# Splitting the conv half of the output weights on GpSimd instead of ScalarE and VectorE, in the late stages of an RWKV-7 and short-convolution block

## The chip, the core and the metric

The kernel runs on one core of a Trainium2 chip. The metric is the device time of one launch in microseconds (us). The engines are called as the profile calls them: PE (TensorE matmul) with its weight loads PEld, DVE (VectorE), ACT (ScalarE), POOL (GpSimd) and SP (SyncE, which issues most DMAs).

## The reference

One layer is applied to 128 context tokens and to 2048 latent tokens. Both are RMS-normalised, modulated and projected by one matrix. Half of the channels go through RWKV-7 mixing in two directions (a recurrence over the tokens, 8 heads of 64), the other half through a gated short convolution; both halves are gated, joined and sent through one output matrix. What this case touches is the end:

```python
ya = ya.astype(x.dtype) * jax.nn.silu(g_a)
yb = b_gate * _short_conv(c_gate * u_conv, lp['conv_w'], is_latent) * jax.nn.silu(g_b)
u = jnp.concatenate([ya, yb], axis=-1) @ lp['w_out']
return x + gate * u, s_final
```

The inner width is 1024: rows 0 to 511 of `w_out` belong to `ya` (the attention half) and rows 512 to 1023 to `yb` (the conv half). All is float32.

## The kernel before, in words

The kernel has three phases. Phase 1 makes the projections and the whole conv half of the mix, and writes them to DRAM (`mixT` holds the mix, transposed). Phase 2 runs the recurrence in chunks of 64 tokens; phase 3 is the output projection with the final norm.

**Phase 2** has 17 stages (0 to 16): 16 for latent tokens, and the context as stage 15. Each stage has two groups of 8 units (one group for each direction). Its work is cut into parts: `partW` (matmuls psF and psG, masked by DVE at L1041 and L1048, copied by ACT at L831), `partU` (psU, psW), `partB` (psX, copied by ACT at L829; psE, whose one half DVE masks at L1109 and whose other half ACT copies at L831 into the tile E) and `partS` (psS, the recurrence itself, with DVE at L1147). A round does `partS` of stage s beside W, U and B of stage s+1; the order of the pieces is a string written out by hand (ROUND, and ROUND_END from stage 14 on), and the matmuls of phase 2 are chained in that order on PE. `finish` (psT, L1195 to L1217) ends a block of the mix. GpSimd's own work in phase 2 is a triangular solve for each stage (`solve`, L935 to L955); the last one ends before the late stages.

**Phase 3** multiplies tiles of 128 tokens by the output matrix. A float32 matmul there is made of three products of rounded numbers: each operand is split into a rounded part hi (type fp32r) and the rest lo = x - hi, and hi*hi, hi*lo and lo*hi are summed (L1380 to L1382). So every block of 128 rows of weights (k = 0 to 7, of 128x1024) is loaded as `woraw`, rounded into `woh` (`load_k`, L1360) and subtracted into `wol` (L1361); every tile's mix is loaded as `mx`, rounded into `mh` (`load_m`, L1372) and subtracted into `ml` (L1373). CONV is k = 4 to 7, ATT is k = 0 to 3.

**The work done ahead.** `ahead` (L1392) does part of phase 3 in the late stages of phase 2: it splits the four conv blocks of weights, and then the conv half of the mixes of tiles 5 and 6 (AHEAD), multiplies these (psa, 24 matmuls a tile) and keeps the result in `z0`. The tiles that hold the split weights are reused from phase 2: woh4 and wol4 take the place of stage 13's operands, woh5 and wol5 that of stage 14's, so they can be written only when the psF and psG matmuls of that stage are over. The buffers `raw` are two: woraw4 and woraw5 are loaded early, and woraw6, woraw7, mxc5 and mxc6 each take a buffer that an earlier subtraction has released. The attention half is split later, by `tail`, with ACT at L1360 and POOL at L1361.

A scheduler places all these instructions into each engine's one queue; every engine works its queue in order. The DMAs of `woraw` (L1354) and `mx` (L1369) stand in SP's queue between the loads of phase 2, of which those of `fg` (`load_half`, L998 and L1001) are the many.

Of the kernel before, what the change touches and what calls it, by code (L numbers as in the profile page):

```python
# [6 lines left out]
F32 = mybir.dt.float32  # L7
F32R = mybir.dt.float32r
BF16 = mybir.dt.bfloat16
AF = mybir.ActivationFunctionType  # L10
ALU = mybir.AluOpType
# [1328 lines left out]
def phase3(K):  # L1340
    nc, tc, A, S = K.nc, K.tc, K.A, K.S
    V, G, P, T = nc.vector, nc.gpsimd, nc.scalar, nc.tensor
    D = nc.sync.dma_start
    O = Ctx()
    wk = {}
    CONV, ATT = (4, 5, 6, 7), (0, 1, 2, 3)
    TILES = [5, 6, 7, 8, 9, 10, 11, 12, 0, 13, 14, 15, 16, 1, 2, 3, 4]
    AHEAD = TILES[:2]
    z0 = {}

    def load_raw(k):

        raw = O.r.tile([128, 1024], F32, tag="raw", name=f"woraw{k}", bufs=2)
        D(raw[:], A["wout"][k * 128:(k + 1) * 128, :])  # L1354
        return raw

    def load_k(k, hi, lo, eng, raw=None):

        raw = raw or load_raw(k)
        P.copy(hi[:], raw[:])  # L1360
        eng.tensor_tensor(lo[:], raw[:], hi[:].bitcast(F32), ALU.subtract)  # L1361
        wk[k] = (hi, lo)

    def load_m(pool, i, ks, b):

        t0 = i * 128
        a = "c" if ks is CONV else "a"
        mx = O.r.tile([128, 4, 128], F32, tag="raw", name=f"mx{a}{i}", bufs=2)
        D(mx[:], S["mixT"].rearrange("(k p) t -> p k t", p=128)[:, ks[0]:ks[0] + 4, t0:t0 + 128])  # L1369
        mh = pool.tile([128, 4, 128], F32R, tag=f"mh{a}", name=f"mh{a}{i}", bufs=b)  # L1370
        ml = pool.tile([128, 4, 128], F32R, tag=f"ml{a}", name=f"ml{a}{i}", bufs=b)
        P.copy(mh[:], mx[:])  # L1372
        V.tensor_tensor(ml[:], mx[:], mh[:].bitcast(F32), ALU.subtract)  # L1373
        return mh, ml

    def products(ps, ms, cs, ks, start, stop):
        mh, ml = ms
        for n, k in enumerate(ks):
            hi, lo = wk[k]
            T.matmul(ps[:], mh[:, n], hi[:, cs], start=start and n == 0, stop=False)  # L1380
            T.matmul(ps[:], mh[:, n], lo[:, cs], start=False, stop=False)  # L1381
            T.matmul(ps[:], ml[:, n], hi[:, cs], start=False, stop=stop and n == 3)  # L1382

    HALF = [slice(0, 512), slice(512, 1024)]

    def weights():
        O.r = Pool(K, "p3r", "left")
        O.pr = Pool(K, "p3pr", "right", 2, PSUM)
        O.pu = O.pr
        O.raw = [load_raw(k) for k in CONV[:2]]  # L1390

    def ahead():  # L1392
        yield
        for n, k in enumerate(CONV):
            load_k(k, *[K.spare(f"wo{a}{k}", F32R, f"o{k - 3}{m}") if n < 2 else O.r.tile([128, 1024], F32R, name=f"wo{a}{k}") for m, a in enumerate("hl")], V, O.raw[n])
            if n < 2:
                O.raw.append(load_raw(CONV[n + 2]))
            yield
        for i in AHEAD:
            ms = load_m(O.r, i, CONV, 1)  # L1400
            if i not in z0:
                z0[i] = K.spare(f"z0_{i}", F32, "ab2" if z0 else "ab")
            for h in range(2):
                ps = O.pr.tile([128, 512], F32, tag="u", name=f"psa{i}_{h}")
                products(ps, ms, HALF[h], CONV, True, True)
                P.copy(z0[i][:, HALF[h]], ps[:])
                yield

    def tail():
        O.l = Pool(K, "p3l", "right")  # L1410
        for k in ATT:
            load_k(k, *[K.spare(f"wo{a}{k}", F32R, ("o00", "o01", "o30", "o31", "zb")[k * 2 + n]) if k * 2 + n < 5 else O.l.tile([128, 1024], F32R, name=f"wo{a}{k}") for n, a in enumerate("hl")], G)
        gb = O.l.tile([128, 2, 1024], F32, name="gb")
        for s in range(2):
            D(gb[:, s], S["gate"][s:s + 1, :].broadcast_to((128, 1024)))
        fg = O.l.tile([128, 1024], F32, name="fg")
        D(fg[:], A["fg"].broadcast_to((128, 1024)))
        eps = O.l.tile([128, 1], F32, name="eps3")
        V.memset(eps[:], 1e-6)
        yield  # L1420

        def tl(shape, tag, i, dt=F32, b=2):
            return O.l.tile(shape, dt, tag=tag, name=f"{tag}{i}", bufs=b)

        for i in TILES:
            t0 = i * 128
            mc = load_m(O.r, i, CONV, 1) if i not in z0 else None
            assert K.mixed[(i - 1) // 4 if i else None] == (4 if i else 1)
            ma = load_m(O.l, i, ATT, 2)
            xt = tl([128, 1024], "x3", i)  # L1430
            D(xt[:], A["x"][t0:t0 + 128, :])
            z = tl([128, 1024], "z", i)
            s = 1 if i == 0 else 0
            ss = tl([128, 2], "ss", i)
            sq = tl([128, 512], "sq", i, b=1)
            last = i == TILES[-1]
            for n, cs in enumerate(HALF):
                ps = O.pu.tile([128, 512], F32, tag="u", name=f"psu{i}_{cs.start}")
                if mc:
                    products(ps, mc, cs, CONV, True, False)  # L1440
                products(ps, ma, cs, ATT, not mc, True)
                if mc:
                    V.tensor_tensor(z[:, cs], ps[:], gb[:, s, cs], ALU.mult)  # L1443
                else:
                    V.tensor_tensor(z[:, cs], ps[:], z0[i][:, cs], ALU.add)
                    V.tensor_tensor(z[:, cs], z[:, cs], gb[:, s, cs], ALU.mult)
                (V if last else G).tensor_tensor(z[:, cs], z[:, cs], xt[:, cs], ALU.add)  # L1447
                P.activation(sq[:], z[:, cs], AF.Square, accum_out=ss[:, n:n + 1])
            V.tensor_tensor(ss[:, 0:1], ss[:, 0:1], ss[:, 1:2], ALU.add)
            P.activation(ss[:, 0:1], ss[:, 0:1], AF.Sqrt, bias=eps[:], scale=1.0 / 1024)  # L1450
            V.reciprocal(ss[:, 0:1], ss[:, 0:1])
            for cs in HALF if last else [slice(0, 1024)]:
                V.scalar_tensor_tensor(z[:, cs], z[:, cs], ss[:, 0:1], fg[:, cs], ALU.mult, ALU.mult)
                D(S["y"][t0:t0 + 128, cs], z[:, cs])
            yield

    def rest(gen):
        O.pl = Pool(K, "p3pl", "left", 6, PSUM)
        O.pu = O.pl
        for _ in gen:  # L1460
            pass
        for p in (O.pl, O.pr, O.l, O.r):
            p.close()

    K.weights, K.ahead, K.tail, K.rest = weights, ahead, tail, rest


# [43 lines left out]
```

## Time and profile before

| what | value |
|---|---|
| median of 3 runs | 1651.52 us (1651.35 to 1659.19) |
| the profiled execution | 1657.8 us, its span 1656.0 us |
| busy share of the span | PE 93%, PEld 85%, DVE 67%, ACT 46%, POOL 34% |
| mean granted clock of PE | 0.969 |

In the profile, the window views give for a stretch of time the busy us of each engine, the granted clock of PE (1.00 is full speed), the busy share of the DMA engines and GB/s. A timeline's row gives start, length, engine, line, operation, tiles and count, and in brackets the idle time ahead of it with what ended it. Late stages are here those from 1322 us on: psa is worked from 1373.72 to 1393.66 us, and the tiles' own loop of phase 3 starts at 1466.21 us and runs to the end.

### The profile page before, as it was taken

The numbers are of one execution on the slowest core, as the hardware profiler recorded it, in microseconds if no ns is written. First come the engines' busy times: TensorE is split into PE (matmuls) and PEld (weight loads), VectorE is DVE, ScalarE is ACT, GpSimd is POOL, SyncE is SP. The second block draws the span as 40 slices with busy tenths as digits, with TensorE's granted clock in tenths as the row PEclk, the third lists the DMA queues.
The fourth block names the chain that finished last, engine by engine and source line by source line (L and its number), as shares of the span: only waits on it lengthen the run. The fifth ranks groups of instructions, "written<-read, shape, count | busy, mean of one in ns | idle before, by whom it ended". The sixth has DMA issues, their size and how long they took to land.

```text
span 1656.0 us, 42386 instructions
## 1 busy us (share of the span) xinstructions
PE 1538.7 (93%) x17160; PEld 1412.4 (85%) x17160; DVE 1108.4 (67%) x2226; ACT 766.8 (46%) x1623; POOL 569.0 (34%) x1028
## 2 busy tenths in 40 slices
PE   5899999999999999999999899988988888789998
PEld 2899998999999999999988898878887777668886
DVE  5876977784738775658787883576775765574333
ACT  4544565553425353435554013667675665432222
POOL 0011211110102121112765564888888700022221
PEclk8899999999999999999999999999999989889999
DMA  9677767664746465655858768676767643264342
GB/s 377 205 263 249 244 234 276 218 225 178 241 140 208 166 207 183 200 202 186 271 165 270 237 201 239 179 192 180 204 175 195 169 131 102 66 198 160 127 149 93
DMA packets 237988, 327.23 MB, mean 198 GB/s; under 512 B 91288, under 2 KB 191896, under 8 KB 223712
## 3 DMA queue, kind: packets, MB, share of 16 engines
q1 hardware_dynamic: 231840, 318.55, 60.8%
q0 software_dynamic: 1200, 3.93, 0.6%
q8 instruction: 135, 2.21, 0.6%
q10 hardware_dynamic: 4752, 2.04, 0.5%
q14 instruction: 61, 0.50, 0.1%
HBM read 207.92 MB, written 116.54 MB: 196 GB/s over the span
## 4 chain that ended last, share of the span: by engine, by line
PE 47%; DVE 10%; ACT 7%; DMA 4%; issue 3%; POOL 3%; SPq 0%; DVEq 0%; ACTq 0%; POOLq 0%
PE psu L1380 4%; PE psu L1381 4%; PE psu L1382 4%; PE psE L840 3%; PE psS L840 2%; ACT fg L829 2%; PE psX L840 2%; PE psW L840 1%; PE mmg L166 1%; PE mmg L168 1%; PE mmg L167 1%; PE mmc L166 1%; PE mmc L167 1%; PE mmu L167 1%; PE mmu L166 1%
## 5 line engine op out<-in xcount | busy, mean ns | idle before, releaser
L950 POOL TENSOR_TENSOR zt<-zt,ztmp 128x30 f32<-128x30 f32 (+7 forms) x390 | 153.3, 393 | 30.6
L840 PE MATMUL psE<-fg 128*64 128x128 f32 x2176 | 135.8, 278 | 17.4 <-ACT fg L831 15.2
L840 PEld LDWEIGHTS psE<-fg 128*64 128x64 f32 x2176 | 120.8, 139 | 24.1 <-ACT fg L831 17.8
L840 PE MATMUL psS<-sv,E 128*64 128x64 f32 x2176 | 99.5, 235 | 19.3 <-DVE sv L1147 18.4
L840 PEld LDWEIGHTS psS<-sv,E 128*64 128x64 f32 x2176 | 82.5, 144 | 35.5 <-DVE sv L1147 24.4
L329 POOL TENSOR_TENSOR shk<-rawl 128x384 f32<-128x384 f32 (+1 forms) x24 | 24.8, 1033 | 242.9 <-ACT rawl L325 223.8
L829 ACT ACTIVATE fg<-psX 64x512 f32<-64x512 f32 x136 | 80.4, 591 | 44.9 <-PE psX L840 42.8
L1147 DVE TENSOR_TENSOR sv<-psS,pc 64x128 f32<-64x128 f32 x254 | 63.9, 277 | 43.6 <-PE psS L840 41.4
L947 POOL TENSOR_TENSOR ztmp<-ab,zt 128x60 f32<-128x60 f32 (+4 forms) x165 | 85.1, 516 | 12.9
L1447 POOL TENSOR_TENSOR z<-z,x 128x512 f32<-128x512 f32 x32 | 41.7, 1304 | 138.3 <-DVE z L1443 114.8
L329 POOL TENSOR_TENSOR shv<-rawl 128x384 f32<-128x384 f32 (+1 forms) x24 | 20.8, 866 | 164.5 <-ACT rawl L325 164.4
L1041 DVE TENSOR_TENSOR F<-psF,consts 128x512 f32<-128x512 f32 x68 | 44.0, 681 | 46.5 <-PE psF L840 46.5
L831 ACT COPY fg<-psG 64x256 f32<-64x256 f32 x136 | 49.8, 366 | 52.4 <-DVE fg L1048 46.3
L1048 DVE TENSOR_TENSOR fg<-psG,consts 64x256 f32<-64x256 f32 x136 | 57.3, 421 | 24.0 <-ACT fg L831 11.7
L166 PE MATMUL mmc<-h,w 128*128 128x384 f32 (+1 forms) x192 | 64.8, 337 | 5.9 <-ACT q1r L327 4.1
L446 POOL COPY pcs<-pp 128x6 f32<-128x6 f32 (+1 forms) x48 | 21.0, 437 | 139.2 <-ACT pp L435 138.9
L166 PE MATMUL mmg<-h,w 128*128 128x384 f32 (+1 forms) x192 | 64.3, 335 | 3.8 <-ACT q1v L327 3.8
L831 ACT COPY E<-psE 128x256 f32<-128x256 f32 x136 | 48.4, 373 | 37.8 <-DVE E L1109 27.9
L1109 DVE TENSOR_TENSOR E<-psE,consts 128x256 f32<-128x256 f32 x136 | 53.0, 418 | 19.0 <-PE psE L840 17.6
L166 PE MATMUL mmb<-h,w 128*128 128x384 f32 (+1 forms) x192 | 62.9, 328 | 1.5 <-ACT ta L439 1.5
L166 PE MATMUL mmgb<-h,w 128*128 128x384 f32 (+1 forms) x192 | 64.0, 333 | 0.3 <-ACT q1r L327 0.3
L168 PE MATMUL mmg<-h,w 128*128 128x384 f32 (+1 forms) x192 | 64.0, 334 | 0.0
(323 smaller groups left out, 5173.3 us busy)
## 6 DMA issues: line engine op xcount, KB each, us to landing
w<-scr_wsp SPq DMA_DIRECT2D x68, 1024.0 KB, 5.7
scr_wsp<-w SPq DMA_DIRECT2D x34, 1024.0 KB, 4.9
scr_ops<-pair SPq DMA_DIRECT2D x80, 384.0 KB, 4.0
wr<-in_win SPq DMA_DIRECT2D x34, 512.0 KB, 5.9
o<-scr_ops SPq DMA_DIRECT2D x32, 512.0 KB, 6.6
fg<-scr_ops SPq DMA_DIRECT2D x120, 128.0 KB, 3.5
x<-in_x SPq DMA_DIRECT2D x17, 512.0 KB, 8.5
wadas<-in_wada SPq DMA_DIRECT2D x8, 1024.0 KB, 13.5
```

The lines of the kernel that those rows point to most:

```text
L166: T.matmul(ps[:, :n], w[:, 0, k], hh[:, 0, k, :n], start=k == 0, stop=False)
L168: K.dense = T.matmul(ps[:, :n], w[:, 1, k], hh[:, 0, k, :n], start=False, stop=k == 7).ins
L829: P.activation(dst, src, AF.Copy, scale=-1.0)
L831: P.copy(dst, src)
L840: r = T.matmul(*a, start=True, stop=True, **k)
L947: eng.tensor_tensor(tv, ab[:, j:j + 2, j + 2:32].unsqueeze(1).broadcast_to((128, kn, 2, n)), zt[:, :kn, j:j + 2].unsqueeze(3).broadcast_to ...
L950: last = eng.tensor_tensor(zt[:, :kn, j + 2:32], zt[:, :kn, j + 2:32], tv[:, :, r], ALU.subtract).ins
L1048: V.tensor_tensor(g.gs[H[1 - h], g.op, h, us], ps[gi][r, :, 64:128], B.mG[r, g.d].unsqueeze(1).broadcast_to((64, 4, 64)), ALU.mult)
L1147: r = V.tensor_tensor(dst, sp[gi][0:64, q], B.pc[0:64, d, 2 * p:2 * p + 2, c:c + 1].broadcast_to((64, 2, 64)), ALU.mult)
L1380: T.matmul(ps[:], mh[:, n], hi[:, cs], start=start and n == 0, stop=False)
L1381: T.matmul(ps[:], mh[:, n], lo[:, cs], start=False, stop=False)
L1382: T.matmul(ps[:], ml[:, n], hi[:, cs], start=False, stop=stop and n == 3)
```

## The change

`load_k` copies with GpSimd when it is given a `raw` tile, which only `ahead` does, and `ahead` hands GpSimd to it for the subtraction as well; `load_m` gets the engines as arguments, and `ahead` passes GpSimd for both. So twelve instructions move: four casts of 128x1024 (ACT, L1360) and four subtractions of 128x1024 (DVE, L1361), two casts of 128x512 (ACT, L1372) and two subtractions of 128x512 (DVE, L1373), all to POOL. The attention half and the other 15 tiles are as they were. Lines from 1359 on are one higher after the change.

```diff
     def load_k(k, hi, lo, eng, raw=None):
 
+        copy = P.copy if raw is None else G.tensor_copy
         raw = raw or load_raw(k)
-        P.copy(hi[:], raw[:])
+        copy(hi[:], raw[:])
         eng.tensor_tensor(lo[:], raw[:], hi[:].bitcast(F32), ALU.subtract)
...
-    def load_m(pool, i, ks, b):
+    def load_m(pool, i, ks, b, copy=P.copy, eng=V):
...
-        P.copy(mh[:], mx[:])
-        V.tensor_tensor(ml[:], mx[:], mh[:].bitcast(F32), ALU.subtract)
+        copy(mh[:], mx[:])
+        eng.tensor_tensor(ml[:], mx[:], mh[:].bitcast(F32), ALU.subtract)
...
         for n, k in enumerate(CONV):
-            load_k(k, *[...], V, O.raw[n])
+            load_k(k, *[...], G, O.raw[n])
...
-            ms = load_m(O.r, i, CONV, 1)
+            ms = load_m(O.r, i, CONV, 1, G.tensor_copy, G)
```

The scheduler then orders the queues anew. On POOL, behind the last solve, this is the difference (woh4 is the rounded block k = 4, sv are the states that phase 2 clears for stage 15, mhc5 and mlc5 are the two parts of tile 5's mix):

```order
 L955 DMA scr_zt_66<-zt_1124_15938 128x512
+L1361 CAST woh4_17891<-woraw4_17735 128x1024
+L1362 TENSOR_TENSOR wol4_17892<-woraw4_17735,woh4_17891 128x1024
+L1361 CAST woh6_17947<-woraw6_17895 128x1024
+L1362 TENSOR_TENSOR wol6_17948<-woraw6_17895,woh6_17947 128x1024
+L1361 CAST woh7_17998<-woraw7_17933 128x1024
+L1362 TENSOR_TENSOR wol7_17999<-woraw7_17933,woh7_17998 128x1024
 L970 MEMSET sv_1207_17780 64x128 x4
+L1373 CAST mhc5_18060<-mxc5_18058 128x512
 L970 MEMSET sv_1208_17786 64x128 x4
+L1361 CAST woh5_17929<-woraw5_17737 128x1024
+L1374 TENSOR_TENSOR mlc5_18061<-mxc5_18058,mhc5_18060 128x512
```

Blocks 4, 6 and 7 come first, then the parts of tile 5 mixed with the memsets, then block 5; wol5, mhc6 and mlc6 follow.

On DVE, in the round in which stage 13's E is made (psE13 with group and piece), two pieces of the difference show the places of wol6 and mlc5:

```order
 L1109 TENSOR_TENSOR E_1182_17259<-psE13_1_00_17260,consts_9809 128x4x64
 L1109 TENSOR_TENSOR E_1181_17247<-psE13_0_01_17271,consts_9809 128x4x64
-L1361 TENSOR_TENSOR wol6_17948<-woraw6_17895,woh6_17947 128x1024
 L1109 TENSOR_TENSOR E_1182_17259<-psE13_1_01_17282,consts_9809 128x4x64
 L1041 TENSOR_TENSOR F_1190_17359<-psF14_0_0_17341,consts_9809 128x512
```

```order
 L1147 TENSOR_TENSOR sv_1168_16901<-psS13_1_0_17395,pc_10967 64x128
 L1109 TENSOR_TENSOR E_1193_17403<-psE13_0_11_17437,consts_9809 128x4x64
-L1373 TENSOR_TENSOR mlc5_18061<-mxc5_18058,mhc5_18060 128x512
 L1109 TENSOR_TENSOR E_1194_17415<-psE13_1_11_17448,consts_9809 128x4x64
 L1147 TENSOR_TENSOR sv_1167_16899<-psS13_0_0_17389,pc_10967 64x128
```

Each subtraction stood between two masks of E, and is gone from there; the rest keeps its order, but for three masks at L1048, which come one or two places earlier.

On SP, the loads of `woraw6`, `woraw7` and the mixes move against the loads of `fg` for stage 15:

```order
 L987 DMA sv_1188_17336<-scr_vt_60 64x1024
-L1354 DMA woraw6_17895<-in_wout 128x1024
 L1001 DMA fg0_9816<-scr_ops0_57 64x2x128 x4
 L1001 DMA fg1_9817<-scr_ops1_58 64x2x128 x4
+L1354 DMA woraw6_17895<-in_wout 128x1024
+L1001 DMA fg0_9816<-scr_ops0_57 64x2x128 x3
 L1354 DMA woraw7_17933<-in_wout 128x1024
-L1369 DMA mxc5_18058<-scr_mixT_63 128x4x128
-L1001 DMA fg0_9816<-scr_ops0_57 64x2x128 x4
+L1001 DMA fg0_9816<-scr_ops0_57 64x2x128
 L1001 DMA fg1_9817<-scr_ops1_58 64x2x128 x4
-L1369 DMA mxc6_18169<-scr_mixT_63 128x4x128
```

`woraw6` now comes behind the eight loads of fg's first half, `woraw7` stands among those of its second half, and both mixes are loaded later, behind `zc` and the gate loads of a block. On PE, the same 48 products of psa stand at the same place in phase 2's order, at stage 15's psF; those that need mlc5 and wol5 have moved some places back among them.

More of the change, by code (lines that the diff above doesn't have):

```diff
@@ L1394, in ahead @@
         for n, k in enumerate(CONV):
-            load_k(k, *[K.spare(f"wo{a}{k}", F32R, f"o{k - 3}{m}") if n < 2 else O.r.tile([128, 1024], F32R, name=f"wo{a}{k}") for m, a in enumerate("hl")], V, O.raw[n])
+            load_k(k, *[K.spare(f"wo{a}{k}", F32R, f"o{k - 3}{m}") if n < 2 else O.r.tile([128, 1024], F32R, name=f"wo{a}{k}") for m, a in enumerate("hl")], G, O.raw[n])
             if n < 2:
```

## The prediction

> **What bounds the kernel now.** I read the page first, then the busy time by stretches, then the timelines of PE, ACT, DVE and SP in the late stages. Each stretch below runs from one psU to the next, which is one round (columns: length, busy us of PE, PEld, DVE, ACT, POOL with counts, granted clock, DMA share, GB/s).
>
> ```profile
> span 1656.0 us, 42386 instructions
> ```
>
> ```profile
> 1298.80:1322.00 23.20, 21.47 (x585) 19.37 (x580) 18.40 (x45) 15.00 (x32) 15.97 (x35) 1.00 0.69 186
> 1322.00:1353.90 31.90, 25.30 (x586) 21.87 (x583) 20.20 (x47) 20.65 (x40) 0.00 (x0) 0.89 0.47 126
> 1353.90:1394.30 40.40, 38.05 (x632) 31.64 (x630) 18.05 (x45) 21.11 (x42) 1.26 (x8) 0.87 0.37 102
> ...
> 1341.30:1348.10 6.80, 6.13 (x80) 5.00 (x74) 4.43 (x9) 5.63 (x10) 0.00 (x0) 0.50 0.36 98
> ...
> 1355.00:1361.70 6.70, 6.70 (x137) 5.95 (x132) 3.26 (x7) 3.54 (x6) 0.00 (x0) 0.50 0.55 154
> ...
> 1372.00:1375.40 3.40, 3.40 (x39) 2.78 (x29) 0.22 (x1) 2.35 (x5) 0.00 (x0) 0.51 0.63 187
> ```
>
> The first round holds no work of phase 3 and ran at full clock: 23.2 us. The second has the same matmuls (586 against 585) and took 31.9. POOL stood idle in it, while ACT and DVE carried 5.7 and 1.8 us more. In three stretches of 6.8, 6.7 and 3.4 us PE had half its clock. PE's timeline shows where the time goes:
>
> ```profile
> 1298.85 1.20 PE L840 MATMUL psU<-zr,a 32*32 32x32 f32 x64
> ...
> 1308.97 3.71 PE L840 MATMUL psE<-fg 128*64 128x128 f32 x64
> ...
> 1313.54 1.05 PE L840 MATMUL psF<-fg,o 64*64 64x128 f32 x32
> ...
> 1315.00 1.09 PE L840 MATMUL psG<-fg,o 64*64 64x128 f32 x28 [0.19 <-ACT fg L829]
> ...
> 1316.53 1.92 PE L840 MATMUL psE<-fg 128*64 128x128 f32 x32
> ...
> 1322.00 1.20 PE L840 MATMUL psU<-zr,a 32*32 32x32 f32 x64
> ...
> 1332.22 2.84 PE L840 MATMUL psE<-fg 128*64 128x128 f32 x48
> 1336.18 1.09 PE L840 MATMUL psE<-fg 128*64 128x128 f32 x16 [1.12 <-ACT fg L831]
> ...
> 1340.31 1.58 PE L840 MATMUL psF<-fg,o 64*64 64x128 f32 x32 [2.00 <-ACT E L831]
> ...
> 1343.26 1.97 PE L840 MATMUL psG<-fg,o 64*64 64x128 f32 x28 [0.53 <-ACT fg L829]
> ...
> 1346.06 2.94 PE L840 MATMUL psE<-fg 128*64 128x128 f32 x32
> ...
> 1353.25 0.69 PE L840 MATMUL psS<-sv,E 128*64 128x64 f32 x16 [1.57 <-DVE sv L1147]
> 1353.87 1.20 PE L840 MATMUL psU<-zr,a 32*32 32x32 f32 x64
> ...
> 1365.81 2.84 PE L840 MATMUL psE<-fg 128*64 128x128 f32 x48
> 1370.65 1.09 PE L840 MATMUL psE<-fg 128*64 128x128 f32 x16 [2.00 <-ACT fg L831]
> ...
> 1373.15 0.65 PE L840 MATMUL psF<-fg,o 64*64 64x128 f32 x4
> ```
>
> PE is the engine that works through the late stages in order, and four times it waits for 1.12 to 2.00 us on ACT or DVE. The rows of ACT just ahead of these waits say what held it:
>
> ```profile
> 1333.11 1.04 ACT L1360 CAST woh<-woraw 128x1024 fp32r<-128x1024 f32 x1
> ...
> 1338.94 1.04 ACT L1360 CAST woh<-woraw 128x1024 fp32r<-128x1024 f32 x1 [1.89 <-DMA woraw<-in_wout]
> ...
> 1351.33 0.62 ACT L1372 CAST mhc<-mxc 128x512 fp32r<-128x512 f32 x1 [1.02 <-DMA mxc<-scr_mixT]
> ...
> 1367.19 1.04 ACT L1360 CAST woh<-woraw 128x1024 fp32r<-128x1024 f32 x1
> ```
>
> ```profile
> 1351.98 0.69 DVE L1373 TENSOR_TENSOR mlc<-mxc,mhc 128x512 fp32r<-128x512 f32 x1 [1.17 <-ACT mhc L1372]
> 1352.59 0.42 DVE L1109 TENSOR_TENSOR E<-psE,consts 128x256 f32<-128x256 f32 x1
> ```
>
> A cast does not only cost its 1.04 us. The second one stood in ACT's queue for 1.89 us until its weights landed, with copies of E behind it, and PE's psF waited for these. In the same way DVE held a mask of E behind mlc, which waited for mhc, which waited for a load.
>
> **What the change takes away.** The twelve instructions leave ACT and DVE, and with them the waits for DMA in the middle of the recurrence's chain. I price it by comparison with the clean round. There psE came 10.12 us after psU (1308.97 less 1298.85), psF 4.57 after that, the next psU 8.46 after that. In the late rounds the same steps took 10.22, 8.09 and 13.56 us, then 11.94 and 7.34. The excess is 0.10 + 3.52 + 5.10 + 1.82 + 2.77 = 13.3 us up to 1373.15, where psa begins. Of the twelve, all but the cast and the subtraction of tile 6 stand ahead of that point; these two fell beside psa.
>
> Of the 13.3 us, half clock made 0.88 (1.97 against 1.09 for 28 psG), 1.02 (2.94 against 1.92 for 32 psE) and the 1.82 of the step from psU to psE, whose matmuls had no wait of more: 3.7 us. The other 9.6 us are waits and what follows from them. These I count whole, since the first round shows that nothing else in such a round holds PE for long. The half clock follows a wait each time: after the 2.00 us ahead of 1340.31, and after the 1.57 us ahead of 1353.25. Without these waits it should go, but where such a stretch falls may differ from one execution to the next, and the profiled execution is 6.3 us above the median of the timed runs (1657.8 against 1651.52), by what is not shown. So I count half, 1.9 us, and keep 0 and 3.7 for the range.
>
> The Trainium skill (TensorE: Matmul & The Clock Gate, Part 1: The HAM clock gate) has it that a free-running activity window of about 3.4 us decides on half or full clock; the stretches of 6.8, 6.7 and 3.4 us agree as two, two and one of them. By that rule the term is a matter of how the windows fall, anywhere between nothing and all of it.
>
> **What it adds.** POOL now makes all of it, one after another, and SP's queue stands between. The rows for the prices:
>
> ```profile
> L1361 DVE TENSOR_TENSOR wol<-woraw,woh x4: 1173/1225/1226, 1334.2 to 1368.3; 128x1024 fp32r<-128x1024 f32 x4
> L1361 POOL TENSOR_TENSOR wol<-woraw,woh x4: 2336/2346/2778, 1406.5 to 1456.5; 128x1024 fp32r<-128x1024 f32 x4
> ```
>
> ```profile
> L970 POOL MEMSET sv<- x8: 194/196/198, 1364.1 to 1365.4; 64x128 f32 x8
> ```
>
> ```profile
> L935 POOL MEMSET zt<- x13: 524/529/533, 900.7 to 1289.0; 128x512 f32 x13
> ```
>
> ```profile
> L1129 POOL COPY sv<-held x2: 283/285/287, 1402.3 to 1403.3; 64x128 f32<-64x128 f32 x2
> ```
>
> ```profile
> 1335.43 0.34 SPq L1354 DMA_DIRECT2D woraw<-in_wout  x1
> 1335.87 5.20 SPq L1001 DMA_DIRECT2D fg<-scr_ops  x8
> 1341.27 0.43 SPq L1354 DMA_DIRECT2D woraw<-in_wout  x1
> ...
> 1348.36 0.38 SPq L1369 DMA_DIRECT2D mxc<-scr_mixT  x1
> ```
>
> The subtraction takes 2.35 us on POOL against 1.22 on DVE, and I take 1.2 for the half-sized one. No cast runs on POOL before. Twice the memset of 128x512 is 1.06 us, and a two-input subtraction is 2.35: the price c of a cast of 128x1024 lies between them. A copy of 64x128 took 285 ns where a memset of that size took 196, 1.45 times as much, and 1.45 times 1.06 is the 1.5 us I take; it is nearer the memset, since a copy too has less to read than the subtraction.
>
> The Trainium skill (GPSIMD Engine Reference, 4.1 Engine selection) speaks against this change: elementwise work of two inputs belongs on VectorE, as GpSimd is about twice as slow, and with one input it is roughly at line rate. The trace agrees on the first (2.35 against 1.22), and no row shows the second; at the page's 1.2 GHz, 1024 elements would be an estimated 0.85 us, and by that POOL would hardly be late at all and the gain 11.5.
>
> The chain on POOL, in the time of before: woh4 can start when psG of stage 13 ends, at 1332.3, and wol4 ends at 1332.3 + 1.5 + 2.35 = 1336.2. SP now issues woraw6 behind the eight fg loads (5.20 us, from some 1335.2), at 1340.4, and it lands 3.5 us later, as before (1335.43 to 1338.94). wol6 ends at 1347.8. Only then woraw7 can go, with five fg loads queued behind it, which stage 15 reads late; it lands at 1351.3, and wol7 ends at 1355.2. mxc5 lands at 1358.2 (2.97 us, as 1348.36 to 1351.33), and mhc5 ends at 1358.9. With a memset (0.63 for four pieces, estimated at 0.8) woh5 ends at some 1361.2, mlc5 at 1362.4 and wol5 at 1364.8. woh5 waits besides for psG of stage 14, which by then is over.
>
> PE, moved by 13.3, would come to psa at 1360.4. It has four products of woh4 and wol4 (0.23 us each):
>
> ```profile
> 1376.70 0.40 PE L1380 MATMUL psa<-woh,mhc 128*128 128x512 f32 x1
> 1376.93 0.39 PE L1381 MATMUL psa<-wol,mhc 128*128 128x512 f32 x1
> ```
>
> At 1361.3 it then waits 1.1 us for mlc5, does four more and 16 matmuls of phase 2, and waits another 0.9 us for wol5: late by 2.0 us. Each microsecond more for c adds 3.5 us (woh6, woh7, woh5 and half of one for mhc5), so the bounds of c give 0.5 and 5.0. In front of phase 2's matmuls stands psa on PE, so this lateness holds up everything. Tile 6 is not late: PE needs mhc6 some 10 us later, and POOL has 2.7 us to do for it.
>
> **The sum.** 9.6 + 1.9 - 2.0 = 9.5 us; I take 9.2 and leave the rest for waits that show up behind those removed. The profiled execution would go from 1657.8 to 1648.6, and the median from 1651.5 to 1642.3 us. From 1394 on everything hangs on PE and on what PE releases, so all of it moves forward by the same.
>
> **The rivals.** *The clock is not won.* The waits go, but half clock falls elsewhere: none of the 3.7 us comes back, and one more window of half the 6.8 us costs 1.7: 9.6 - 2.0 - 1.7 = 5.9, or 1645.6 us. For it speaks that the 1.57 us wait was enough for 6.7 us at 0.50; against it, that the clean round has waits below half of that and the clock at 1.00.
>
> *POOL is late.* If c is at the subtraction's 2.35, PE waits 5.0 us ahead of psa and falls to half clock there, which costs another 1.9, and none of the old clock term counts: 9.6 - 5.0 - 1.9 = 2.7, or 1648.8 us. The two-input rows of POOL speak for it, the memset against it.
>
> *Slower than before.* psa stands in PE's order ahead of the rest of stage 15, and PE can't pass it. If a cast to fp32r runs as a slow routine on POOL, the chain that ends in wol5 decides: the gain is gone where the lateness reaches 11.5 us, at c = 1.5 + (11.5 - 2.0) / 3.5 = 4.2 us, and it is 0.5% slower at 6.6. At 7 it would be 1651.5 + 9.8 = 1661.3 us. Against it speaks that POOL writes fp32r in its subtractions at 2.35 us with two inputs.
>
> **How the numbers follow.** About 0.5%, or 8.3 us, is what a measurement of this kernel can tell from no change. The forecast has 0.68: most of it (0.53) gains over 8.3 us, 0.15 ends just below. The clock rival has 0.18 and the late POOL 0.10, both within 0.5%; slower has 0.04. So faster 0.53, same 0.43, slower 0.04. The low end takes all of the clock and the small c, 9.6 + 3.7 - 0.5 = 12.8, and 1.2 of the up to 1.7 us that the stretch of 3.4 us at 0.51, at the start of psa, can have cost: 14, or 1637.5. The high end is the late POOL's 1648.8 and a microsecond: 1650.
>
> **What would show it.** The rounds from psU to psU should fall from 31.9 to some 24 and from 40.4 to some 36 us, with no row of L1361 or L1373 on ACT among them and no wait of PE on ACT's E beyond the clean round's. POOL's casts should show c at 1.5; PE should wait about 1 us each for mlc5 and wol5 at psa. If PE waits over 4 us there, POOL's price or the SP queue is what I had wrong. If the waits go and the clock's stretches of 0.50 are as long as before, it is the clock term. If the waits stay with other releasers, the clean round was the wrong measure.

## The result, and the profile after

| | before | after |
|---|---|---|
| median | 1655.84 us (1650.61 to 1661.42, 14 runs) | 1646.63 us (1640.42 to 1662.37, 14 runs) |
| profiled execution, its span | 1657.8, 1656.0 us | 1644.25, 1642.5 us |
| mean granted clock | 0.969 | 0.974 |
| busy share ACT, POOL | 46%, 34% | 46%, 36% |

The ratio is 0.9954, with a 95% interval of 0.9939 to 0.9970: a gain of 0.46%, or 7.6 us (5.0 to 10.1); the two medians lie 9.2 us apart. The forecast was a gain of 9.2, to 1642.3 us, in a range of 1637.5 to 1650. It was counted from three runs of the kernel before with a median of 1651.5 us; the median of the 14 runs is 4.3 us higher, so the gain is the fairer thing to compare.

First the rounds of the kernel after, from psU to psU, as in the prediction's first window view, then the stretch at psa:

```profile
1314.70:1337.96 23.26, 21.57 (x584) 19.42 (x580) 16.08 (x43) 17.33 (x36) 4.48 (x5) 1.00 0.54 148
1337.96:1378.57 40.61, 36.48 (x633) 29.68 (x629) 16.21 (x43) 19.70 (x40) 14.85 (x18) 0.92 0.47 122
1378.57:1410.33 31.76, 24.54 (x567) 21.38 (x564) 18.83 (x45) 15.66 (x33) 2.92 (x3) 0.89 0.28 77
1410.33:1453.40 43.07, 29.08 (x608) 24.74 (x605) 27.54 (x69) 19.16 (x37) 7.44 (x3) 0.85 0.44 143
1355.00:1361.60 6.60, 5.70 (x40) 3.91 (x40) 0.00 (x0) 1.47 (x3) 5.24 (x8) 0.50 0.43 102
```

In the kernel before, the two rounds that the prediction didn't show were these:

```profile
1394.30:1423.13 28.83, 23.84 (x567) 20.67 (x565) 18.70 (x45) 15.62 (x33) 2.91 (x3) 0.94 0.32 84
1423.13:1466.21 43.08, 28.80 (x609) 24.46 (x605) 27.52 (x69) 19.14 (x37) 7.43 (x3) 0.86 0.45 142
```

The first late round fell from 31.9 to 23.3 us: it is now the clean round. The second did not move (40.4, 40.6), the third grew by 2.9, the fourth stayed, and the rest of the span went from 189.8 to 189.1. From the psU at 1322.0 (now 1314.7) to the end the sum is 334.0 against 327.8: 6.2 us won. That psU itself came 7.3 us earlier, with no moved instruction ahead of it (5.2 us of this lie in the round from stage 11 to 12: 30.3 us at a granted clock of 0.89 before, 25.1 at 1.00 after); the difference of the two spans, 13.5 us, is therefore not all due to the change, and the ratio's 7.6 fits the 6.2.

The gain of the second round is there, and is given back inside it. PE's timeline, second late round of the kernel after:

```profile
1337.96 1.20 PE L840 MATMUL psU<-zr,a 32*32 32x32 f32 x64
...
1348.05 3.71 PE L840 MATMUL psE<-fg 128*64 128x128 f32 x64
...
1352.63 0.39 PE L840 MATMUL psF<-fg,o 64*64 64x128 f32 x4
1355.19 0.80 PE L1381 MATMUL psa<-woh,mhc 128*128 128x512 f32 x1 [2.17 <-POOL mhc L1373]
1355.78 0.63 PE L1382 MATMUL psa<-wol,mhc 128*128 128x512 f32 x1
1356.21 0.63 PE L1381 MATMUL psa<-woh,mhc 128*128 128x512 f32 x1
...
1357.98 0.80 PE L1383 MATMUL psa<-woh,mlc 128*128 128x512 f32 x1 [0.71 <-POOL mlc L1374]
...
1359.98 1.76 PE L840 MATMUL psF<-fg,o 64*64 64x128 f32 x26
...
1378.57 1.20 PE L840 MATMUL psU<-zr,a 32*32 32x32 f32 x64
```

Up to psF PE needs 14.67 us from psU, as in the clean round (14.69), where the kernel before needed 19.3. From there to the next psU it takes 25.9 against 21.1: 4.8 us lost. It waits 2.17 us for mhc5 and 0.71 for mlc5, and in the 6.6 us from the first of these on the clock is 0.50: the products start 0.43 us apart (1355.78 to 1356.21) instead of 0.23.

Why mhc5 is late stands in POOL's timeline and in SP's:

```profile
1344.80 1.04 POOL L1361 CAST woh<-woraw 128x1024 fp32r<-128x1024 f32 x1 [3.81 <-DMA woraw<-in_wout]
1345.92 2.69 POOL L1362 TENSOR_TENSOR wol<-woraw,woh 128x1024 fp32r<-128x1024 f32 x1
...
1354.53 0.61 POOL L1373 CAST mhc<-mxc 128x512 fp32r<-128x512 f32 x1 [5.34 <-DMA mxc<-scr_mixT]
```

```profile
1348.87 0.39 SPq L1370 DMA_DIRECT2D mxc<-scr_mixT  x1
1349.37 1.29 SPq L989 DMA_DIRECT2D sv<-scr_vt  x2
1350.75 2.66 SPq L998 DMA_DIRECT2D fg<-scr_ops  x4
```

mxc5 goes out as soon as wol7 has released its buffer (1348.61), and lands 5.7 us later, beside other loads. POOL stands idle for it. In the kernel before the same load took 2.97 us. That the loads beside it make it longer is inferred from the DMA share (the figure ahead of GB/s) over the load's time, before and after:

```profile
1348.36:1351.33 2.97, 2.97 (x70) 2.97 (x68) 2.30 (x7) 1.44 (x4) 0.00 (x0) 1.00 0.33 94
```

```profile
1348.87:1354.53 5.66, 4.15 (x90) 3.73 (x86) 2.61 (x7) 4.36 (x11) 0.32 (x4) 1.00 1.04 229
```

The casts themselves are cheap. The group rows of the two casts in the kernel after, ns least, median and most:

```profile
L1361 POOL CAST woh<-woraw x4: 1030/1035/1038, 1325.1 to 1355.7; 128x1024 fp32r<-128x1024 f32 x4
L1361 ACT CAST woh<-woraw x4: 1027/1038/1051, 1392.0 to 1442.1; 128x1024 fp32r<-128x1024 f32 x4
```

GpSimd rounds a block in 1.04 us, as ScalarE does; the forecast had taken 1.5.

### The profile page after: what moved, and what is told of

It is laid out like the page before. It is cut to its first block, busy times and chain, and to the rows that moved or that the text cites. A ratio compares the mean times of both kernels' runs of the same rounds, so it can differ in the third digit from the quotient of the medians.

```text
span 1642.5 us, 42385 instructions
## 1 busy us (share of the span) xinstructions
PE 1531.9 (93%) x17160; PEld 1405.2 (86%) x17160; DVE 1104.6 (67%) x2220; ACT 762.7 (46%) x1617; POOL 586.8 (36%) x1040
## 4 chain that ended last, share of the span: by engine, by line
PE 45%; POOL 9%; DVE 8%; ACT 4%; issue 4%; DMA 3%; SPq 0%; DVEq 0%; POOLq 0%; ACTq 0%
POOL zt L950 4%; PE psu L1381 4%; PE psu L1382 4%; PE psu L1383 4%; POOL ztmp L947 3%; PE psE L840 2%; PE psS L840 2%; ACT fg L829 1%; PE mmc L166 1%; PE mmg L168 1%; PE mmg L166 1%; PE mmg L167 1%; PE mmc L167 1%; PE mmc L168 1%; PE mmv L166 1%
## 5 line engine op out<-in xcount | busy, mean ns | idle before, releaser
L950 POOL TENSOR_TENSOR zt<-zt,ztmp 128x30 f32<-128x30 f32 (+7 forms) x390 | 153.0, 392 | 30.6
L840 PEld LDWEIGHTS psS<-sv,E 128*64 128x64 f32 x2176 | 81.6, 143 | 34.8 <-DVE sv L1147 24.9
L829 ACT ACTIVATE fg<-psX 64x512 f32<-64x512 f32 x136 | 80.5, 592 | 37.3 <-PE psX L840 35.2
L1048 DVE TENSOR_TENSOR fg<-psG,consts 64x256 f32<-64x256 f32 x136 | 57.4, 422 | 25.1 <-ACT fg L831 11.2
L166 PE MATMUL mmg<-h,w 128*128 128x384 f32 (+1 forms) x192 | 63.6, 331 | 3.8 <-ACT q1v L327 3.8
L831 ACT COPY E<-psE 128x256 f32<-128x256 f32 x136 | 48.5, 373 | 36.8 <-DVE E L1109 27.4
L166 PE MATMUL mmv<-h,w 128*128 128x384 f32 (+1 forms) x192 | 63.4, 330 | 0.3 <-ACT q1r L327 0.3
## 6 DMA issues: line engine op xcount, KB each, us to landing
wadas<-in_wada SPq DMA_DIRECT2D x8, 1024.0 KB, 13.5
```

Source lines behind the costliest of these rows:

```text
L166: T.matmul(ps[:, :n], w[:, 0, k], hh[:, 0, k, :n], start=k == 0, stop=False)
L829: P.activation(dst, src, AF.Copy, scale=-1.0)
L831: P.copy(dst, src)
L840: r = T.matmul(*a, start=True, stop=True, **k)
L950: last = eng.tensor_tensor(zt[:, :kn, j + 2:32], zt[:, :kn, j + 2:32], tv[:, :, r], ALU.subtract).ins
L1048: V.tensor_tensor(g.gs[H[1 - h], g.op, h, us], ps[gi][r, :, 64:128], B.mG[r, g.d].unsqueeze(1).broadcast_to((64, 4, 64)), ALU.mult)
```

## The experiments

The theory after this result: **A**, ACT and DVE lost most of their time not on their own work for the splits but on waiting in their queues for loads, and GpSimd wins since nothing else is queued behind it; what is given back comes from mxc5's place in the loads. The rival, **B**: the splits are dear on ACT and DVE as work, and POOL's chain is what makes psa late.

All rounds in one table (us, from psU to psU; stage numbers at the top, "tail" is the first psu of phase 3; the sum runs from the psU of stage 13 to the end and adds the rounded rounds). The ratios of the experiments (4 to 12 runs of a kernel) are against runs of the kernel before beside them, with medians of 1655.23, 1654.86 and 1654.80 us.

| kernel | 13-14 | 14-15 | 15-16 | 16-tail | tail-end | sum | ratio (95%) |
|---|---|---|---|---|---|---|---|
| before | 31.9 | 40.4 | 28.9 | 43.1 | 189.8 | 334.1 | 1 |
| after | 23.3 | 40.6 | 31.8 | 43.1 | 189.1 | 327.9 | 0.9954 (0.9939 to 0.9970) |
| weights_only | 23.3 | 44.4 | 31.6 | 43.0 | 189.1 | 331.4 | 0.9979 (0.9965 to 0.9994) |
| mixes_only | 29.1 | 36.1 | 30.7 | 42.7 | 189.4 | 328.0 | 0.9978 (0.9964 to 0.9991) |
| casts_only | 28.5 | 34.7 | 26.4 | 42.8 | 189.1 | 321.5 | 0.9917 (0.9893 to 0.9940) |
| before_raw3 | 24.2 | 36.1 | 30.4 | 33.3 | 192.5 | 316.5 | 0.9973 (0.9952 to 0.9994) |
| after_raw3 | 23.3 | 34.7 | 31.1 | 33.4 | 192.6 | 315.1 | 0.9973 (0.9957 to 0.9988) |
| before_mid3 | 24.5 | 36.1 | 29.1 | 33.4 | 192.4 | 315.5 | 0.9971 (0.9953 to 0.9989) |
| after_mid3 | 23.3 | 34.7 | 31.0 | 33.4 | 192.5 | 314.9 | 1.0085 (1.0062 to 1.0107) |
| before_midown | 30.2 | 36.1 | 31.5 | 35.2 | 191.7 | 324.7 | 0.9947 (0.9927 to 0.9966) |
| casts_midown | 27.4 | 38.5 | 28.4 | 35.7 | 191.8 | 321.8 | 1.0157 (1.0119 to 1.0196) |
| after_midown | 23.3 | 34.8 | 30.4 | 34.6 | 191.7 | 314.8 | 0.9903 (0.9878 to 0.9928) |
| after_midown2 | 23.3 | 35.0 | 30.6 | 35.7 | 191.5 | 316.1 | 0.9907 (0.9882 to 0.9932) |

**One half of the change at a time.** In weights_only the mixes go back to ACT and DVE:

```diff
-            ms = load_m(O.r, i, CONV, 1, G.tensor_copy, G)
+            ms = load_m(O.r, i, CONV, 1)
```

> The change for the four weight blocks alone; mhc and mlc of tiles 5 and 6 are on ACT and DVE again. Theory A: mxc5's load still stands behind wol7, so psa is as late as in the changed kernel, and now ACT and DVE wait for it in their queues too; the first late round near 23.3 us, the second 40 to 42, the ratio 0.995 to 0.998. If the two mixes on POOL were what makes psa late (POOL's own work), the second round falls to some 38 us and the ratio to 0.993.

In mixes_only the weights go back:

```diff
-        copy = P.copy if raw is None else G.tensor_copy
+        copy = P.copy
...
-            load_k(k, *[...], G, O.raw[n])
+            load_k(k, *[...], V, O.raw[n])
```

> The change for the mixes of tiles 5 and 6 alone; the weight blocks stay on ACT and DVE. Theory A: the stall of ACT on woraw6 (1.89 us) and the casts of blocks 4 and 5 stay, the stall of DVE's E behind mlc5 goes: first late round 28 to 30 us in place of 31.9, second as before (40.4), ratio 0.997 to 0.9985.

The first late round shows it plainly: 23.3 with the weights on POOL, 29.1 without. In the second, weights_only is the worst of all, 44.4, where 40 to 42 was expected. Its ACT waits for the same late load, with the copies of E and fg behind it:

```profile
1361.21 0.62 ACT L1373 CAST mhc<-mxc 128x512 fp32r<-128x512 f32 x1 [8.03 <-DMA mxc<-scr_mixT]
```

So the lateness of mxc5 comes with the weights' split on POOL, and having POOL wait for it instead of ACT is worth 3.8 us (44.4 to 40.6). In mixes_only the load is not late, and the round is 36.1, where the 40.4 of the kernel before was expected.

The first late round of mixes_only is also the best measure here of work against waiting. It has three blocks of weights on ACT and DVE, as the kernel before has, ran at full clock, and holds one wait of ACT for a load:

```profile
1318.49:1347.62 29.13, 22.87 (x585) 19.51 (x581) 19.42 (x46) 20.11 (x39) 0.17 (x1) 1.00 0.48 134
```

```profile
1335.23 1.04 ACT L1361 CAST woh<-woraw 128x1024 fp32r<-128x1024 f32 x1 [1.82 <-DMA woraw<-in_wout]
```

The round is 5.9 us longer than one without splits on these engines (29.1 against 23.3). If the wait costs its whole 1.8, some 4 us are left for three blocks: an estimated 1.4 us of work a block.

**The casts alone.** casts_only leaves the six subtractions on DVE:

```diff
-            load_k(k, *[...], G, O.raw[n])
+            load_k(k, *[...], V, O.raw[n])
...
-            ms = load_m(O.r, i, CONV, 1, G.tensor_copy, G)
+            ms = load_m(O.r, i, CONV, 1, G.tensor_copy)
```

> Only the six casts go to POOL; the six subtractions stay on DVE. Theory A: ACT is freed, but DVE still holds masks of E behind wol6 and mlc5, which now wait for POOL's cast, which waits for the load: the first late round stays at 28 to 32 us, the second at 39 to 42, ratio 0.997 to 1.000. If ACT's queue alone was the cost, the first late round falls to 24 to 25 us and the ratio is near that of the whole change, 0.9955.

The first round came as expected (28.5). DVE now stood there for the cast, which waited on POOL for a load:

```profile
1337.57 1.23 DVE L1362 TENSOR_TENSOR wol<-woraw,woh 128x1024 fp32r<-128x1024 f32 x1 [3.73 <-POOL woh L1361]
```

The second missed: 34.7 where 39 to 42 was expected, and the kernel beat the whole change. (The third late round, 26.4 against 31.8, adds 5.4 to its lead, and the first takes 5.2 back.) In its order of SP's queue mxc5 stands ahead of zc and not behind it, and psa starts with no wait, at full clock (SP, then PE):

```profile
1345.89 0.38 SPq L1370 DMA_DIRECT2D mxc<-scr_mixT  x1
1346.37 2.55 SPq L1001 DMA_DIRECT2D fg<-scr_ops  x4
...
1350.81 0.60 SPq L1027 DMA_DIRECT2D zc<-scr_zt  x1
```

```profile
1361.69 0.39 PE L840 MATMUL psF<-fg,o 64*64 64x128 f32 x4
1362.00 0.50 PE L1381 MATMUL psa<-woh,mhc 128*128 128x512 f32 x1
1362.34 0.40 PE L1382 MATMUL psa<-wol,mhc 128*128 128x512 f32 x1
```

In these kernels the second round goes with when mxc5 is loaded, and an edit elsewhere moves that. after_midown, below, puts this to the test.

**One more raw buffer.** The same edit was made to the kernel after (after_raw3) and to the kernel before (before_raw3):

```diff
-        raw = O.r.tile([128, 1024], F32, tag="raw", name=f"woraw{k}", bufs=2)
+        raw = O.r.tile([128, 1024], F32, tag="raw", name=f"woraw{k}", bufs=3)
...
-        mx = O.r.tile([128, 4, 128], F32, tag="raw", name=f"mx{a}{i}", bufs=2)
+        mx = O.r.tile([128, 4, 128], F32, tag="raw", name=f"mx{a}{i}", bufs=3)
```

> The changed kernel with three buffers for the raw loads in place of two, so that woraw6, woraw7, mxc5 and mxc6 are loaded some 300 us earlier and blocks 6 and 7 and tile 5 are split before the late rounds; twelve instructions stay on POOL. Theory A (the gain of the change is the waits of ACT and DVE for loads in rounds 13 and 14, and some 4.8 us of it are given back because psa waits on PE for mxc5, whose load stands behind wol7): round psU(13) to psU(14) stays near 23.3 us, psU(14) to psU(15) falls from 40.6 to some 36 us, PE waits under 0.5 us for POOL at psa, and the time is 4 to 5 us below the changed kernel, a ratio to before near 0.9925. Theory B (what was won is chance in the clock, the waits at psa cost nothing in the end): same as the changed kernel, near 0.9955.

> The kernel before with three raw buffers, all splitting still on ACT and DVE; the loads are early, so no cast waits for a DMA in the late rounds. Theory A1 (the wait for loads in the queues of ACT and DVE is the cost, not the work itself): the round psU(13) to psU(14) falls from 31.9 to 24 to 25 us, psU(14) to psU(15) from 40.4 to 37 to 39, and the ratio is near 0.994 or better, as good as the changed kernel without GpSimd. Theory A2 (the work of 1.04 and 1.22 us a block is itself on the chain): woh4, wol4, woh5 and wol5 still stand there, each pair costs 1 to 2 us, and the ratio is 0.996 to 0.998.

Without GpSimd the late rounds are almost as short (24.2 and 36.1) as with it (23.3 and 34.7). This does not part waiting from work, though: in both kernels blocks 6 and 7 and tile 5 are split long before, and only one block is left in each late round. In before_raw3 ACT waits for no load there, and a block costs 1.1 us in the first round (24.23 against 23.17 in the round ahead of it) and 1.3 in the second (36.08 against 34.74 in after_raw3):

```profile
1028.39 1.04 ACT L1360 CAST woh<-woraw 128x1024 fp32r<-128x1024 f32 x1 [13.32 <-DMA woraw<-in_wout]
...
1341.40 1.04 ACT L1360 CAST woh<-woraw 128x1024 fp32r<-128x1024 f32 x1
1365.46 1.04 ACT L1360 CAST woh<-woraw 128x1024 fp32r<-128x1024 f32 x1
```

But the scheduler takes the new buffer to load and split at the start of phase 2, and there ACT stands 13.32 us for a load: the psU of stage 1 came 14 us later than in the kernel before (1033.4 against 1019.6). In after_raw3 the rounds ahead of the late ones took some 11 us more than in the kernel before, with splits on POOL between its solves. Both kept only 0.27%, where ratios of 0.9925 for after_raw3 and 0.994 or better for before_raw3 were expected.

**The loads placed by hand.** after_mid3 and before_mid3 are these two with all loads of raw data ordered behind the first matmul of stage 8, and the splits behind the last solve:

```diff
+            if s == 8:
+                K.mid = K.first
...
-        D(raw[:], A["wout"][k * 128:(k + 1) * 128, :])
+        d = D(raw[:], A["wout"][k * 128:(k + 1) * 128, :])
+        order(d, K.mid)
...
-        copy(hi[:], raw[:])
+        order(copy(hi[:], raw[:]), K.solved)
```

The same goes for `mx` and `mh`; `order` only tells the scheduler. after_midown goes back to two raw buffers, and gives the mixes two of their own (`tag="mxr"`), with the same ordering.

> The changed kernel with three raw buffers, its loads standing in SP's queue from stage 8 on, POOL's splits behind the last solve: the late half of the three-buffer kernel without its work at the start of phase 2 and without splits among the solves. Theory: from psU(13) to the end it stays as fast as with three buffers loaded early (315 us against 334 before), and the 11 us that this kernel lost between psU(2) and psU(13) do not come: some 1638 us, a ratio of 0.988 to 0.991. Rival (the loads cost the same wherever they stand): 0.996 to 0.998.

> The kernel before with the same three raw buffers and the same placing of the loads, the splits on ACT and DVE. It differs from its partner only in the engine that splits. Theory A1 (loads waited for in the queues were the cost): within 0.1% of its partner. Theory A2 (ACT's and DVE's own work on the chain costs too): 2 to 4 us slower than its partner, from psU(13) to psU(15) 60.3 us as with early loads, where the partner has 58.

> The changed kernel, where the mixes of tiles 5 and 6 have two buffers of their own in place of sharing the two raw ones, so that mxc5 no longer waits for wol7; all raw loads stand in SP's queue from stage 8 on and not at the start of phase 2, and POOL's splits stand behind the last solve. Theory A (psa was late because mxc5's load waited for wol7 and then ran beside the loads of phase 2): PE's waits for mhc5 and mlc5 at psa go, psU(14) to psU(15) falls from 40.6 to 36 to 37 us, the round before stays at 23.3, the sum from psU(13) to the end falls by 4 us from 327.9, the ratio to before is 0.992 to 0.9945. Theory C (POOL's own work, wol5 above all, makes psa late): the round stays at 39 to 41, the ratio at 0.995 to 0.9965.

after_mid3 was 0.85% slower than the kernel before, by a stall of its own: its round from stage 12 to 13 took 55.2 us. SP's queue, then PE's:

```profile
1283.38 0.34 SPq L1185 DMA_DIRECT2D w<-scr_q  x1
1321.71 0.35 SPq L1360 DMA_DIRECT2D woraw<-in_wout  x1
...
1323.18 2.63 SPq L998 DMA_DIRECT2D fg<-scr_ops  x4
```

```profile
1328.04 2.21 PE L840 MATMUL psF<-fg,o 64*64 64x128 f32 x14 [16.34 <-DMA fg<-scr_ops]
```

For 37.9 us SP stood on a load of weights for which no buffer was free, until POOL's subtraction behind the last solve ended (1319.33 and 2.35 us), and the loads of fg stood behind it. before_mid3 has a smaller stall, a round of 40.3 from stage 11 to 12, with a wait of ACT:

```profile
1288.58 1.04 ACT L1367 CAST woh<-woraw 128x1024 fp32r<-128x1024 f32 x1 [6.04 <-DMA woraw<-in_wout]
```

The two late rounds up to the psU of stage 15 took 60.7 us together in before_mid3 and 58.0 in after_mid3. So the two blocks that ACT and DVE split there without waiting cost 2.7 us, which is what the expectation's theory A2 had and not A1.

after_midown has no such stall, and it has the lowest ratio of all, 0.9903 (0.9907 when run again), though the interval of casts_only overlaps with it. mxc5 is there long ahead, and psa starts without a wait:

```profile
1356.84 0.39 PE L840 MATMUL psF<-fg,o 64*64 64x128 f32 x4
1357.15 0.50 PE L1389 MATMUL psa<-woh,mhc 128*128 128x512 f32 x1
```

From psF to the next psU it takes 20.1 us, against 25.9 in the kernel after, with the splits on GpSimd in both. So it was the late load that held up psa, and not GpSimd's own work. With the added buffers the tail comes sooner too, as in the kernels with three raw buffers: 34.6 us from the psU of stage 16, against 43.1, of which the longer tail takes back 2.6. The load of the tail's first mix and the first product, in after_midown (SP, PE) and in the kernel after:

```profile
1421.18 0.37 SPq L1377 DMA_DIRECT2D mxa<-scr_mixT  x1
```

```profile
1442.01 0.50 PE L1389 MATMUL psu<-woh,mha 128*128 128x512 f32 x1 [0.36 <-ACT mha L1381]
```

```profile
1443.69 0.38 SPq L1370 DMA_DIRECT2D mxa<-scr_mixT  x1
```

```profile
1453.40 0.79 PE L1381 MATMUL psu<-woh,mha 128*128 128x512 f32 x1 [3.94 <-ACT mha L1373]
```

**The engine, with buffers and places equal.** before_midown is after_midown with all splits on ACT and DVE; casts_midown has the subtractions on DVE. after_midown2 is after_midown again, beside them.

> The buffers and the places of the loads as in after_midown (the mixes in two buffers of their own, all six loads of raw data placed behind the eighth stage's first matmul, the splits behind the last solve), with the splits on ScalarE and VectorE as before the change. Theory A (with the data there early, the waits for loads in ScalarE's and VectorE's queues are gone, and what GpSimd still takes from them is their own work, worth some 1 to 3 us in the first late round): first late round 24 to 27 us, second 35 to 36, time within 0.3% of after_midown, 1638 to 1645 us. Theory B (the splits on the loaded engines are dear in themselves, whatever the data): first late round 29 to 32, time 6 to 9 us above after_midown, ratio to the kernel before 0.994 to 0.997. A stall of a load in SyncE's queue for a buffer that a split frees late would show as a round of 30 us or more ahead of the late ones.

> As after_midown, with the six casts on GpSimd and the six subtractions on VectorE. Theory A (the data being there early, whoever subtracts does so unwaited; GpSimd is relieved of 6 subtractions, VectorE gets 4 x 1.2 + 2 x 0.6 us that lie under TensorE's work): first late round 23.3 to 25, second 34 to 36, time within 0.3% of after_midown. Theory B (VectorE's subtractions stand in the path of psE and psX, as in the kernel before): first late round 26 to 29, time 3 to 6 us above after_midown. after_midown runs again beside it in the next kernel of this call.

> after_midown once more, on the same chip and beside the same runs of the kernel before as the two kernels above, so that the three can be compared: 1637 to 1643 us, ratio 0.988 to 0.993, first late round 23.3, second 34 to 35.

Here B's numbers came, not A's: 30.2 us for the first late round and a ratio of 0.9947 against 0.9907. One reason is that the data was not there for all of it. Only two raw buffers are left for the weights, so woraw6 still comes late, and ACT and DVE wait for it as in the kernel before:

```profile
1337.68 1.04 ACT L1367 CAST woh<-woraw 128x1024 fp32r<-128x1024 f32 x1 [1.68 <-DMA woraw<-in_wout]
```

```profile
1338.76 1.23 DVE L1368 TENSOR_TENSOR wol<-woraw,woh 128x1024 fp32r<-128x1024 f32 x1 [2.50 <-ACT woh L1367]
```

The other is the work itself. Three blocks stand in this round, as in mixes_only (29.1), and 6.7 us of it ran at a granted clock of 0.52. So theory A, that waiting and not work was most of the cost, is not shown. By the sums GpSimd is worth 8.6 us here (324.7 less 316.1), with three blocks and a late load in the first round, and 1.4 with three raw buffers (316.5 less 315.1), with one block in each round and its data there. casts_midown, which A had expected at after_midown's time, took 1679.12 us. Its subtraction of tile 5 stands early in DVE's queue, the cast that it needs behind the last solve on POOL:

```profile
1317.66 0.69 DVE L1382 TENSOR_TENSOR mlc<-mxc,mhc 128x512 fp32r<-128x512 f32 x1 [38.75 <-POOL mhc L1381]
```

That is one round of 68.4 us: the same trap as in after_mid3, in another queue.

## Why the prediction was right, and where it was not

**The clean round as a measure: right.** The excess of 13.3 us up to psa is gone but for 0.1, and no row of L1361 or L1373 on ACT is left in these rounds. How the 13.3 divide into waiting and work is not measured. At 1.1 to 1.4 us a block (before_raw3 and mixes_only), the four blocks that the kernel before splits ahead of psa would be an estimated 4.4 to 5.6 us of work. The rest is waits for loads, the split of tile 5's mix and the half clock.

**The clock term: too small.** Both stretches of half clock ahead of psa went, so all of the 3.7 us came back where I counted 1.9. But a new one came at psa, 6.6 us at 0.50, so the clock rival (half clock falls elsewhere) was right in part.

**The price of a cast: too high.** I took 1.5 us, and it is 1.04, at the memset's bound. With that price my own chain would have made PE only 0.4 us late. The Trainium skill (GPSIMD Engine Reference, 4.1 Engine selection) has one-input work on GpSimd roughly at line rate; the trace agrees in that POOL's cast takes ACT's time, though the estimate from the page, 0.85, was too low.

**The lateness at psa: the step that failed.** I wrote that "mxc5 lands at 1358.2 (2.97 us, as 1348.36 to 1351.33)" and came to 2.0 us. Set back by the 7.3 us of the earlier start, PE came to psa at 1360.3, as forecast (1360.4), and wol7 ended at 1355.9 (1355.2 forecast); but mxc5 landed at 1361.8. Its load, priced from a quiet stretch (DMA share 0.33), ran in a full one (1.04) and took 5.7 us. And I priced the waits at full clock. They were 2.9 us, and the half clock behind them made 1.6 more on the eight products (0.43 less 0.23 each) and 0.8 on 26 psF (1.76 us, against 0.98 in casts_only, whose psa did not wait):

```profile
1367.31 0.98 PE L840 MATMUL psF<-fg,o 64*64 64x128 f32 x26
```

That is 5.3 us. The kernel before had lost a part of this too, at the half clock of its own first products, so that from psF to the next psU the difference is 4.8 us, where I had 2.0. wol5, for which I had a wait of 0.9, was waited for by nobody. Between the eighth product of psa and the ninth, which reads a wol, stand 32 matmuls of phase 2, where I had 16. The late POOL's rival had this course (a wait, then half clock), but from a dear cast; the cause was the load.

**"From 1394 on ... all of it moves forward by the same": wrong by 2.2 us.** The round from stage 15 to 16 grew by 2.9, and the tail gave 0.7 back. PE waits longer there for one psE (kernel before, then after):

```profile
1408.22 4.12 PE L840 MATMUL psE<-fg 128*64 128x128 f32 x48 [3.34 <-ACT fg L831]
```

```profile
1394.88 5.01 PE L840 MATMUL psE<-fg 128*64 128x128 f32 x48 [5.69 <-ACT fg L831]
```

The copy of fg on ACT waits there for a mask on DVE, and ahead of that mask in DVE's queue stands the transpose of zc (before, then after):

```profile
1403.86 0.70 DVE L1055 STREAM_TRANSPOSE zr<-zc 128x512 f32<-128x512 f32 x1
```

```profile
1390.49 0.71 DVE L1055 STREAM_TRANSPOSE zr<-zc 128x512 f32<-128x512 f32 x1 [2.26 <-issue]
```

It starts 9.6 us after the psU of stage 15 in the kernel before and 11.9 in the kernel after. In all 11 kernels that keep this order (all but casts_only and casts_midown) its start, counted from that psU, less PE's wait is 6.2 us. So the transpose sets the wait. The loads of zc, which it reads, are issued at the same places in both kernels, 3.7 and 5.1 us after that psU. That they landed later is inferred, since the profile names no releaser, and why they did stays open. It is not GpSimd as such: before_midown has a round of 31.5 and before_raw3 one of 30.4 with no split on POOL.

Together: 13.3 won, less 4.8, less 2.9, plus 0.7, is the 6.2 or 6.3 us of the profile. I had 9.5: the clock term gave 1.8 more than I counted, and the other two steps took 2.8 and 2.2 more. That the time came out near the forecast is therefore in part luck. The interval of the gain, 5.0 to 10.1 us, holds the forecast's 9.2 and the clock rival's 5.9 alike; it is the rounds that tell, and the second, forecast at some 36 us, stayed at 40.6.

## What to carry over

Before moving work to another engine, see how much of its cost is work and how much is standing in a queue for data. A wait costs what is queued behind it: on an idle engine nothing unless TensorE needs the result (as it did mhc5), on ScalarE or VectorE the copies that TensorE needs, on SyncE every later load. And where two raw buffers feed a chain of loads, moving the splits moves the loads: look at where each next load then falls, and at what runs beside it.

## What the runs showed of the hardware

GpSimd rounds 128x1024 to fp32r in 1.04 us, ScalarE's time, while its two-input subtraction of that size takes 2.35 against VectorE's 1.22. A wait of TensorE of 2.17 us, and one of 1.57 in the kernel before, was followed by 6.6 and 6.7 us at a granted clock of 0.50; but the first late round of mixes_only has a wait of 1.93 us, and stayed at 1.00:

```profile
1336.60 1.36 PE L840 MATMUL psF<-fg,o 64*64 64x128 f32 x32 [1.93 <-ACT E L831]
```

So the length of one wait does not decide. The Trainium skill (TensorE: Matmul & The Clock Gate, Part 1: The HAM clock gate) puts the drop after an idle window of about 3.4 us; the length of the stretches agrees with two such windows, but the waits ahead of them were shorter than one. A load of a tile's mix took 2.97 us at a DMA share of 0.33, and 5.66 at 1.04.
